# Attention's end and the first branch stage: weights split sooner, loads and splits in program order

## The chip, the core and the metric

The kernel runs on one core of a Trainium2 chip. The metric is the device time of one execution in microseconds (us). The engines named below are TensorE (PE; PEld is its weight load), VectorE (DVE), ScalarE (ACT), GpSimd (POOL), and SyncE (SP), whose queue issues nearly all DMA transfers here. An engine works through its instructions strictly in the order in which they stand in its queue: if one waits, all behind it wait.

## The reference

One layer of a hybrid block over 2048 tokens of width 1024, batch 1, with 256 context tokens, all in float32. Cut to what matters here:

```python
attn_x = merge_heads(attend_blocked(q_x, k_all, v_all))            # 8 heads of 64, 2304 keys
gm_x = gmlp_spatial(gelu(u_x), gelu(vg_x), gm_norm_g, gm_ws, gm_bs)
y = sigmoid(ga_x) * (attn_x @ w_br_attn) + sigmoid(gb_x) * (gm_x @ w_br_gm)   # 512 -> 1024
x = x + g1 * (y @ w_out)                                           # 1024 -> 1024
h2 = modulate(x, norm2_g, sh2, sc2)
x = x + g2 * square(relu(h2 @ w_ff1)) @ w_ff2                      # 1024 -> 4096 -> 1024
```

The softmax of `attend` is divided by its sums late: the kernel stores unscaled attention outputs, the sums, and their reciprocals, and scales when the branch stage reads them.

## The kernel before

**Precision.** A float32 operand is split into a high part (a cast on ACT) and a remainder (a subtraction, here on DVE): `split`, lines 146 and 150. A product is three matmuls, `mm3`, lines 178 (high x high), 179 (high x remainder) and 180 (remainder x high). So the second operand of line 180 needs the remainder of the weight, line 178 only its cast.

**Stages.** Projection, attention, the branch stage with the output product (`merge`), then two feed-forward halves. Tokens come in four blocks of 512.

*Attention* is 16 units (a block and a pair of heads), each of 18 key blocks in three groups of six (`gi` 0 to 2). In a group TensorE does the scores (L1689), ACT the exponentials (L1699), and one group later TensorE the products with the values (L1709) while DVE or POOL add up the exponentials (L1729, L1732; for the last unit all on DVE, its final pair L1718). In the last unit there is no next unit to prepare, and in that time the raw branch weights of m=0 and m=1 (`br_raw`) are loaded and split (`br_weights`): these two sets are `self.ready`.

*The branch stage* of block b runs over m = 0 to 7, the eight 128-wide slices of y. For m, TensorE multiplies the gMLP branch ("g") and the attention branch ("a") by their weights, 12 matmuls each. DVE multiplies each by its gate (L985), adds them (L988), and ACT and DVE split the sum into `y`. Ahead of that, `fetch` loads and splits the weights of two slices later and loads their gates (`gate_in`, L950: `gt<-ta_d`, `gt<-tb_d`). Block 0's stage carries three more things: `load_w_out` loads the eight slices of the output weights (`ws`, L875, 512 KB each) and splits them into `wo`; `last.sums` forms the softmax sums of the last attention unit at m=2; and `last.inverse` turns them into reciprocals through DRAM at m=4 (load L1769, DVE L1770, store L1771).

*The output product* then goes over the four 128-token tiles of the block, two halves of 512 columns each, k = 0 to 7 over the slices of y and `wo`. The first tile runs k = 0 to 6 of both halves first and k = 7 last, so that the last slice may come late. DVE multiplies by g1 (L1032) and adds x (L1033, loaded by L1012), SP stores the result (L1035). Meanwhile the next block's inputs are fetched and split (`br_inputs`, L884, L888, L896).

**Buffers.** At the end of attention the pools `base` and `mid` are closed and `out` and `branch` are opened in the same memory; a tile of a new pool waits for the last user of the bytes below it. `branch` holds 6 gate tiles (`gt`), 14 branch-weight tiles (`bw`; a set is 2 raw and 4 split tiles) and 2 raw output-weight tiles (`ws`). With two `ws` tiles, load k waits until slice k-2 is split. PSUM has 8 banks.

**What sets the order.** A planner puts each engine's instructions in an order of its own, by costs that it assumes, and wait instructions follow from the data. `order`, called at the end of the build, adds edges that hold ranges of the program to program order on their engine:

```python
held = idx in pinned or (idx in fixed and i.engine in engines)      # engines: PE, DVE
held = held or (idx in steady and i.engine != self.nc.sync.engine)  # all but SP
held = held or (idx in loads and i.engine == self.nc.sync.engine)   # SP
```

Attention is in `fixed` (PE and DVE in order, ACT and SP free). `steady` begins at the output product of block 0. Block 0's branch stage is in neither `steady` nor `loads`, so there every queue follows the planner. `loads` holds the second feed-forward product only.

Of the kernel before, what the change touches and what calls it, by code (L numbers as in the profile page):

```python
# [10 lines left out]
F32R = mybir.dt.float32r  # L11
# [7 lines left out]
P = 128  # L19
D = 1024  # L20
KC = D // P
SEQ = 2048
CTX = 256
NH = 8
# [5 lines left out]
TB = 512  # L30
NB = SEQ // TB
TT = TB // P
# [36 lines left out]
class Kern:  # L69
# [748 lines left out]
    def attend(self, units, late):  # L818
        begin = self.here()
        pend, self.ready = [], []  # L820
        for i, u in enumerate(units):
            at = lambda n: units[n] if 0 <= n < len(units) else None
            nxt, far, old, older = at(i + 1), at(i + 2), at(i - 1), at(i - 2)
            for gi, g in enumerate(range(0, NKT, GROUP)):
                group = range(g, g + GROUP)
                step = nxt if gi < 2 else far
                if not nxt and gi == 0:
                    raws = [self.br_raw(m, self.t2) for m in range(2)]
                for j in group:
                    u.scores(j)  # L830
                    if step:
                        step.maxima(1)
                    if gi == 0 and j == 2 and far:
                        far.load()
                if gi == 2 and nxt:
                    nxt.low_queries()
                if gi == 2 and i in FIRST_INPUTS:
                    next(late, None)
                for f in pend:
                    f()  # L840
                if gi == 1 and far:
                    far.queries()
                if gi == 0 and far:
                    far.cast()
                if gi == 2 and old:
                    old.sums()
                if gi == 0:
                    if older:
                        older.inverse()
                    if far:  # L850
                        far.remainder()
                if gi == 1:
                    if nxt:
                        nxt.reference()
                    if old:
                        old.join()
                if gi == 2 and i in FIRST_INPUTS:
                    next(late, None)
                if not nxt and gi:
                    self.ready.append(self.br_weights(raws.pop(0), self.t2))  # L860
                pend = [lambda u=u, j=j: u.values(j) for j in group]
            pend.append(u.leave)
        for f in pend:
            f()
        units[-2].inverse()
        self.fixed.append(range(begin, self.here()))

    def load_w_out(self):
        nc = self.nc
        self.wo = []  # L870
        self.g1b = self.sb("g1", [D])
        nc.sync.dma_start(self.g1b, self.g1_d.partition_broadcast(P)[:, 0, :])
        for k in range(KC):
            st = self.sb("ws", [D])
            nc.sync.dma_start(st, self.I["w_out"][0, k * P : (k + 1) * P, :])  # L875
            h, l = self.sb("wo", [D], F32R), self.sb("wo", [D], F32R)
            self.split(st, h, l, lo_eng="dve")
            self.wo.append((h, l))
            yield

    def br_fetch(self, b, nm, k):
# [72 lines left out]
    def merge(self, first, start, last):  # L954
        nc = self.nc
# [8 lines left out]
        w_out = self.load_w_out()  # L964

        def fetch():
            s = next(it, None)
            if s is not None:
                q.append((self.br_weights(self.br_raw(s[1])), self.gate_in(*s)))

        inp = first
        for ws in self.ready:
            q.append((ws, self.gate_in(*next(it))))
        for b in range(NB):
            y = []
            for m in range(KC):
                fetch()
                ws, gt = q.pop(0)
                for nm in ("g", "a"):
                    ps = self.bank([TB])  # L980
                    wh, wl = ws[nm]
                    for k in range(4):
                        h, l = inp[nm][k]
                        self.mm3(ps, wh[:, k, :], wl[:, k, :], h, l, k == 0, k == 3)
                    nc.vector.scalar_tensor_tensor(  # L985
                        out=gt[nm], in0=gt[nm], scalar=1.0, in1=ps, op0=ALU.add, op1=ALU.mult
                    )
                nc.vector.tensor_tensor(out=gt["a"], in0=gt["a"], in1=gt["g"], op=ALU.add)  # L988
                yh, yl = self.sb("y", [TB], F32R), self.sb("y", [TB], F32R)
                self.split(gt["a"], yh, yl, lo_eng="dve")  # L990
                y.append((yh, yl))
                if b == 0:
                    next(w_out, None)
                    if m == 2:
                        last.sums(self.sb("raw", [TB]))
                    if m == 4:
                        last.inverse()
            inp = {}
            if b == 0:
                begin = self.here()  # L1000
            if b + 1 < NB:
                side = self.br_inputs(b + 1, inp)
            else:
# [5 lines left out]
            for tt in range(TT):  # L1009
                tok = slice(tt * P, (tt + 1) * P)  # L1010
                xt = self.sb("xt", [D])
                nc.sync.dma_start(xt, self.x_block(b)[tok, :])  # L1012
                banks = [self.bank([512]) for _ in range(2)]

                def outer(n, ks):
# [569 lines left out]
class Unit:  # L1585
# [161 lines left out]
    def sums(self, row=None):  # L1747
# [10 lines left out]
        for h in range(2):  # L1758
            n = 2 * self.p + h
            nc.scalar.dma_start(k.sm_d[self.b][n : n + 1], row[h * HD : h * HD + 1])  # L1760

    def inverse(self):
        if self.p + 1 < NH // 2:
            return
        k, nc = self.k, self.nc
        n = NH * TT
        r = (k.sb("raw", [TB]) if self.last else k.t1([P]))[:n, :P]
        pack = lambda d: d.rearrange("h (t c) -> (h t) c", c=P)
        nc.sync.dma_start(r, pack(k.sm_d[self.b]))  # L1769
        nc.vector.reciprocal(r, r)  # L1770
        nc.sync.dma_start(pack(k.rs_d[self.b]), r)  # L1771


@with_exitstack
# [42 lines left out]
```

## Time and profile before

| | |
|---|---|
| median of 3 runs | 3013.18 us (3012.45 to 3016.2) |
| the profiled execution | 3012.34 us; span from first to last instruction 3010.6 us, granted clock 0.999 |
| TensorE busy | 2971.5 us, 99% of the span |
| DVE, ACT, POOL busy | 2024.5 us (67%), 1353.1 us (45%), 564.9 us (19%) |
| attention's last values product | ends near 1395.5 us |
| block 0's branch stage | 1395.5 us to about 1445 us |
| its output product | to about 1489 us |

How to read it: times in the profile are us from the span's start unless marked ns. A row of the timeline has start, length, engine, line, operation, output tile <- input tiles, shapes and count; the bracket at its end is how long the engine stood idle before it and what released it. "SPq" and "ACTq" are the DMA-issuing queues of SP and ACT. In a row of windows each engine's busy time is followed by its number of instructions; then come the granted TensorE clock (1.00 is full), the busy share of the DMA engines, and GB/s. A row of waits has the waiting engine and line, what it waited for, us in total, how often, and the longest. TensorE's matmuls overlap: a row's length is longer than the step from one to the next.

### The profile page before, as it was taken

The page shows a single profiled execution, that of the slowest core. Times are in us where ns is not written, and L with a number is a line of the kernel's source. Part 1 is how long each engine was busy: PE and PEld are TensorE (multiplying, and loading weights), DVE is VectorE, ACT ScalarE, POOL GpSimd, SP SyncE. Part 2 cuts the span into 40 slices and gives each one's busy share as a digit, 9 for nine tenths or more (in the row PEclk, how much of TensorE's full clock was granted, in tenths as well). Part 3 has the DMA queues.
Part 4 walks back from the last instruction along what each step waited for, and adds up shares of the span by engine and source line. Part 5 has one row for each costly group of instructions (what it writes and reads, how often), then busy time and mean ns, then how long its engine had stood idle before and what let it go on. Part 6 is the DMA issues. An engine that isn't in the chain of part 4 may idle for free.

```text
span 3010.6 us, 39824 instructions
## 1 busy us (share of the span) xinstructions
PE 2971.5 (99%) x14973; PEld 2300.4 (76%) x14973; DVE 2024.5 (67%) x2989; ACT 1353.1 (45%) x2041; POOL 564.9 (19%) x420
## 2 busy tenths in 40 slices
PE   7999999999999999999999999999999999999999
PEld 5888888887655656556888878887788888888887
DVE  5848566585777788886655688776755766654455
ACT  4444435342655555554322355443543344444442
POOL 0000000000888899980000000000000000000000
PEclk9999999999999999999999999999999999999999
DMA  7474646643100000003755549888766544446665
GB/s 239 124 219 118 225 137 198 180 138 98 36 15 12 15 19 22 29 26 131 234 174 179 173 151 328 310 305 312 243 203 226 183 154 154 154 148 219 209 218 195
DMA packets 329123, 485.53 MB, mean 161 GB/s; under 512 B 28825, under 2 KB 161217, under 8 KB 328930
## 3 DMA queue, kind: packets, MB, share of 16 engines
q1 hardware_dynamic: 325090, 478.40, 48.1%
q10 hardware_dynamic: 3840, 4.59, 0.4%
q8 instruction: 117, 1.92, 0.3%
q14 instruction: 76, 0.62, 0.1%
HBM read 348.56 MB, written 134.35 MB: 160 GB/s over the span
## 4 chain that ended last, share of the span: by engine, by line
PE 95%; DVE 2%; DMA 2%; ACT 1%; issue 1%; SPq 0%; DVEq 0%; ACTq 0%
PE b L1287 13%; PE b L1288 13%; PE b L1286 13%; PE b L178 11%; PE b L180 11%; PE b L179 11%; PE b L1689 9%; PE b L1709 8%; PE b L1645 2%; PE b L184 2%; DMA w<-in_w_mod 1%; PE b L1751 0%; PE b L288 0%; DMA f<-x_d 0%; DVE ts L1656 0%
## 5 line engine op out<-in xcount | busy, mean ns | idle before, releaser
L1392 DVE TENSOR_TENSOR f<-f,f 128x1024 fp32r<-128x1024 f32 x224 | 264.5, 1221 | 252.7 <-ACT f L1391 252.4
L1656 DVE TENSOR_REDUCE ts<-b 128x1 f32<-128x512 f32 x512 | 311.6, 682 | 105.6 <-PE b L1645 105.5
L1287 PE MATMUL b<-f,f 128*128 128x512 f32 x896 | 350.6, 391 | 5.5 <-DVE f L1392 5.3
L1391 ACT CAST f<-f 128x1024 fp32r<-128x1024 f32 x224 | 224.8, 1052 | 287.3 <-PE b L1287 274.8
L1286 PE MATMUL b<-f,f 128*128 128x512 f32 x896 | 350.2, 391 | 1.3 <-ACT f L1391 1.3
L1288 PE MATMUL b<-f,f 128*128 128x512 f32 x896 | 349.4, 390 | 0.0
L1689 PE MATMUL b<-t,t 64*128 64x512 f32 x2304 | 330.7, 400 | 0.0
L1689 PEld LDWEIGHTS b<-t,t 64*128 64x128 f32 x2304 | 226.1, 184 | 69.2 <-issue 26.1
L1732 POOL TENSOR_TENSOR ac<-ac,p 128x512 f32<-128x512 f32 x204 | 269.0, 1353 | 43.4 <-ACT p L1699 43.4
L1732 POOL TENSOR_TENSOR ac<-ac,t 128x512 f32<-128x512 f32 x146 | 233.2, 1627 | 0.0
L1699 ACT ACTIVATE p<-b 128x512 f32<-128x512 f32 x384 | 206.8, 599 | 48.2 <-PE b L1689 41.4
L1287 PE MATMUL b<-hl,f 128*128 128x512 f32 x576 | 224.4, 390 | 1.8 <-DVE hl L1049 1.8
L1288 PE MATMUL b<-hl,f 128*128 128x512 f32 x576 | 224.1, 389 | 0.0
L1286 PE MATMUL b<-hl,f 128*128 128x512 f32 x576 | 224.1, 389 | 0.0
L150 DVE TENSOR_TENSOR w<-w,w 128x1024 fp32r<-128x1024 f32 x120 | 146.7, 1223 | 113.5 <-ACT w L146 85.7
L178 PE MATMUL b<-t,w 128*128 128x512 f32 x512 | 203.2, 397 | 0.4 <-DVE ts L1651 0.3
L1287 PEld LDWEIGHTS b<-f,f 128*128 128x128 f32 x896 | 168.5, 188 | 44.1 <-DVE f L1392 9.5
L180 PE MATMUL b<-t,w 128*128 128x512 f32 x512 | 199.7, 390 | 0.0
L179 PE MATMUL b<-t,w 128*128 128x512 f32 x512 | 199.5, 390 | 0.0
L1286 PEld LDWEIGHTS b<-f,f 128*128 128x128 f32 x896 | 168.6, 188 | 37.3 <-ACT f L1391 2.4
L1288 PEld LDWEIGHTS b<-f,f 128*128 128x128 f32 x896 | 168.6, 188 | 34.7
L146 ACT CAST w<-w 128x1024 fp32r<-128x1024 f32 x120 | 125.9, 1049 | 146.5 <-DMA w<-in_w_in 116.8
(234 smaller groups left out, 6013.3 us busy)
## 6 DMA issues: line engine op xcount, KB each, us to landing
w<-in_w_in SPq DMA_DIRECT2D x120, 512.0 KB
ao_d<-f SPq DMA_DIRECT2D x224, 256.0 KB
f<-ao_d SPq DMA_DIRECT2D x112, 512.0 KB
f<-w2o_d SPq DMA_DIRECT2D x112, 512.0 KB
f<-in_w_ff SPq DMA_DIRECT2D x48, 1024.0 KB
w2o_d<-f SPq DMA_DIRECT2D x112, 256.0 KB
md<-in_w_mod SPq DMA_DIRECT2D x32, 512.0 KB
f<-x_d SPq DMA_DIRECT2D x64, 256.0 KB
```

The source lines that it names most:

```text
L178: mm(ps, sh, mh, start=start, stop=False, skip_group_check=skip)
L179: mm(ps, sh, ml, start=False, stop=False, skip_group_check=skip)
L180: mm(ps, sl, mh, start=False, stop=stop, skip_group_check=skip)
L1286: mm(ps, wh, hh, start=start and k == 0, stop=False, skip_group_check=True)
L1287: mm(ps, wh, hl, start=False, stop=False, skip_group_check=True)
L1288: mm(ps, wl, hh, start=False, stop=k == len(w) - 1, skip_group_check=True)
L1391: nc.scalar.copy(h, f32(l))
L1392: nc.vector.tensor_tensor(out=l, in0=f32(l), in1=f32(h), op=ALU.subtract)
L1656: nc.vector.tensor_reduce(out=self.mx[:, t, h, c : c + 1], in_=ps[h], axis=AX.X, op=ALU.max)
L1689: self.nc.tensor.matmul(ps[h], keys[h], q[rows[h]], start=n == 0, stop=n == len(steps) - 1, skip_group_check=True,)
L1709: nc.tensor.matmul(self.o[h * HD : (h + 1) * HD, :], k.V[c][:, i, self.kv * HD : (self.kv + 1) * HD], pt[h], start=j == 0, stop=j == NKT - 1,)
L1732: nc.gpsimd.tensor_tensor(out=self.acc[e][:, h], in0=old[:, h], in1=pt[h], op=ALU.add)
```

## The change

Four edits that belong together:

- In the last attention unit the two early branch-weight sets are split after groups 0 and 1, not 1 and 2.
- `load_w_out` issues the load of slice k and then the split of slice k-1, instead of load and split of the same slice; it is stepped twice at m=2 and m=3 (once at every other m), so its last split comes at m=6.
- The reciprocals are formed in two parts: `inverse_in` (the load) at m=4 and `inverse_out` (reciprocal and store) at m=6. The other blocks' reciprocals do both at once as before.
- `begin` moves ahead of block 0's branch stage. So `steady` now holds PE, ACT, DVE and POOL in program order there, and `loads` holds SP in program order from the first gate loads to the end of the stage. The x loads of block 0's output product are pinned, each behind the SP instruction ahead of it in the program.

```diff
--- before.py
+++ after.py
@@ -856,7 +856,7 @@
                         old.join()
                 if gi == 2 and i in FIRST_INPUTS:
                     next(late, None)
-                if not nxt and gi:
+                if not nxt and gi < 2:
                     self.ready.append(self.br_weights(raws.pop(0), self.t2))
                 pend = [lambda u=u, j=j: u.values(j) for j in group]
             pend.append(u.leave)
@@ -870,12 +870,15 @@
         self.wo = []
         self.g1b = self.sb("g1", [D])
         nc.sync.dma_start(self.g1b, self.g1_d.partition_broadcast(P)[:, 0, :])
-        for k in range(KC):
-            st = self.sb("ws", [D])
-            nc.sync.dma_start(st, self.I["w_out"][0, k * P : (k + 1) * P, :])
-            h, l = self.sb("wo", [D], F32R), self.sb("wo", [D], F32R)
-            self.split(st, h, l, lo_eng="dve")
-            self.wo.append((h, l))
+        st = []
+        for k in range(KC + 1):
+            if k < KC:
+                st.append(self.sb("ws", [D]))
+                nc.sync.dma_start(st[k], self.I["w_out"][0, k * P : (k + 1) * P, :])
+            if k:
+                h, l = self.sb("wo", [D], F32R), self.sb("wo", [D], F32R)
+                self.split(st[k - 1], h, l, lo_eng="dve")
+                self.wo.append((h, l))
             yield
 
     def br_fetch(self, b, nm, k):
@@ -969,6 +972,7 @@
                 q.append((self.br_weights(self.br_raw(s[1])), self.gate_in(*s)))
 
         inp = first
+        begin = self.here()
         for ws in self.ready:
             q.append((ws, self.gate_in(*next(it))))
         for b in range(NB):
@@ -990,14 +994,17 @@
                 self.split(gt["a"], yh, yl, lo_eng="dve")
                 y.append((yh, yl))
                 if b == 0:
-                    next(w_out, None)
+                    for _ in range(2 if m in (2, 3) else 1):
+                        next(w_out, None)
                     if m == 2:
                         last.sums(self.sb("raw", [TB]))
                     if m == 4:
-                        last.inverse()
+                        last.inverse_in()
+                    if m == 6:
+                        last.inverse_out()
             inp = {}
             if b == 0:
-                begin = self.here()
+                self.loads.append(range(begin, self.here()))
             if b + 1 < NB:
                 side = self.br_inputs(b + 1, inp)
             else:
@@ -1010,6 +1017,8 @@
                 tok = slice(tt * P, (tt + 1) * P)
                 xt = self.sb("xt", [D])
                 nc.sync.dma_start(xt, self.x_block(b)[tok, :])
+                if b == 0:
+                    self.pins.append((self.here() - 1,))
                 banks = [self.bank([512]) for _ in range(2)]
 
                 def outer(n, ks):
@@ -1759,16 +1768,22 @@
             n = 2 * self.p + h
             nc.scalar.dma_start(k.sm_d[self.b][n : n + 1], row[h * HD : h * HD + 1])
 
+    def inverse_in(self):
+        k = self.k
+        self.sm = (k.sb("raw", [TB]) if self.last else k.t1([P]))[: NH * TT, :P]
+        self.nc.sync.dma_start(self.sm, self.packed(k.sm_d))
+
+    def inverse_out(self):
+        self.nc.vector.reciprocal(self.sm, self.sm)
+        self.nc.sync.dma_start(self.packed(self.k.rs_d), self.sm)
+
+    def packed(self, d):
+        return d[self.b].rearrange("h (t c) -> (h t) c", c=P)
+
     def inverse(self):
-        if self.p + 1 < NH // 2:
-            return
-        k, nc = self.k, self.nc
-        n = NH * TT
-        r = (k.sb("raw", [TB]) if self.last else k.t1([P]))[:n, :P]
-        pack = lambda d: d.rearrange("h (t c) -> (h t) c", c=P)
-        nc.sync.dma_start(r, pack(k.sm_d[self.b]))
-        nc.vector.reciprocal(r, r)
-        nc.sync.dma_start(pack(k.rs_d[self.b]), r)
+        if self.p + 1 == NH // 2:
+            self.inverse_in()
+            self.inverse_out()
 
 
 @with_exitstack
```

## The prediction

> **What bounds the kernel now.** I read the page's busy shares first, then the windows around the change, then each engine's timeline there, then the waits of the DMA-issuing queue SP.
>
> ```profile
> PE 2971.5 (99%) x14973; PEld 2300.4 (76%) x14973; DVE 2024.5 (67%) x2989; ACT 1353.1 (45%) x2041; POOL 564.9 (19%) x420
> ...
> core 0: us, PE busy (x) PEld busy (x) DVE busy (x) ACT busy (x) POOL busy (x), PEclk, DMA share, GB/s
> 1395.00:1480.00 85.00, 81.73 (x353) 64.44 (x350) 57.84 (x82) 28.39 (x43) 0.00 (x0) 1.00 0.76 254
> ...
> 1395.47 0.50 PE L178 MATMUL b<-in,t 128*128 128x512 f32 x1
> ...
> 1407.97 0.50 PE L178 MATMUL b<-in,bw 128*128 128x512 f32 x1 [1.08 <-ACT bw L146]
> ...
> 1410.08 0.51 PE L180 MATMUL b<-in,bw 128*128 128x512 f32 x1 [1.36 <-DVE bw L150]
> ...
> 1433.24 0.50 PE L178 MATMUL b<-in,bw 128*128 128x512 f32 x1 [0.31 <-ACT bw L146]
> ...
> 1434.60 0.50 PE L180 MATMUL b<-in,bw 128*128 128x512 f32 x1 [0.35 <-DVE bw L150]
> ...
> 1439.84 0.50 PE L178 MATMUL b<-in,bw 128*128 128x512 f32 x1 [0.17 <-ACT bw L146]
> ```
>
> TensorE is busy 99% of the span; only its idle time can be won. Block 0's branch stage runs from 1395.47 us; in its window TensorE has 85 - 81.73 = 3.27 us of idle, which is the sum of the five bracketed gaps: 1.08 and 1.36 before the third branch weight (m=2), and 0.31, 0.35 and 0.17 before m=6 and m=7. So 3.27 us, 0.11%, is all the change can win here. POOL is not busy in the stage and no edit issues on it.
>
> ```profile
> SPq L950 <- DVE ac L1729: 78.2, 1, 78.2
> SPq L875 <- DVE wo L150: 6.9, 4, 2.3
> ...
> 1399.32 0.34 SPq L950 DMA_DIRECT2D gt<-ta_d  x1
> ...
> 1401.61 0.51 SPq L934 DMA_DIRECT2D bw<-in_w_br_gm  x1
> ...
> 1390.94 0.62 ACT L146 CAST t<-t 128x512 fp32r<-128x512 f32 x1
> ...
> 1407.31 1.14 ACT L146 CAST bw<-bw 128x512 fp32r<-128x512 f32 x2 [2.34 <-DMA bw<-in_w_br_gm]
> ...
> 1391.60 1.40 DVE L150 TENSOR_TENSOR t<-t,t 128x512 fp32r<-128x512 f32 x2 [12.58 <-ACT t L146]
> ...
> 1397.94 1.23 DVE L1729 TENSOR_TENSOR ac<-ac,t 128x1024 f32<-128x1024 f32 x1
> ```
>
> SP stands idle until its first gate load at 1399.32, released by attention's last sums on DVE (L1729, ends 1399.17). Those were late because DVE waited 12.58 us, in order, for the cast of the second early branch weight (ACT, 1390.94). The third weight, issued at 1401.61, is cast at 1407.31, 0.4 us after TensorE wanted it. From then on SP waits for output-weight splits (L875 behind `wo`).
>
> **The change, part by part.**
>
> *Branch weights a group sooner.* Four casts and four remainders move, nothing is added: 4 x 0.62 us on ACT, 4 x 0.69 us on DVE, now after the first and second groups of the last unit.
>
> ```profile
> 1367.57 0.59 ACT L1739 COPY t<-b 128x512 f32<-128x512 f32 x1 [3.71 <-PE b L1709]
> ...
> 1383.54 2.15 ACT L1699 ACTIVATE t<-b 128x512 f32<-128x512 f32 x4
> ...
> 1359.97 1.23 DVE L1729 TENSOR_TENSOR ac<-p,p 128x1024 f32<-128x1024 f32 x1 [2.78 <-ACT p L1699]
> ...
> 1393.65 1.89 PE L1709 MATMUL b<-t,t 128*64 128x512 f32 x8
> ```
>
> They cost nothing: ACT is idle 3.71 us before 1367.57 and DVE 2.78 us before 1359.97; without that cover TensorE could lose at most the casts' 2.5 us. The last group's exponentials end at 1385.7, so its six sums (1.25 us each) and the final pair end near 1388.5 instead of 1400.5. What holds the gate tile next is TensorE reading the same exponentials: the row at 1393.65 covers the last two key blocks, the first of them done near 1394.7. I take SP's first load there, 4.6 us sooner (at the earliest 1390.5, when the last group's first products are done; at the latest 1395.6). The third weight then lands near 1402.7, before TensorE wants it at 1406.9: the gaps of 1.08 and 1.36 go, a gain of 2.44 us.
>
> *Block 0's stage in order.* Now ACT, DVE and SP keep program order in it. Per m: SP loads the raw weights of m+2, then their gates, then `w_out`; DVE does both remainders of m+2, then m's two gate products, their sum, y's remainder, then the output-weight remainders. What is late next is whatever stands behind the slowest of these. Block 1, already in order on ACT and DVE, gives the chain's length:
>
> ```profile
> 1492.88 1.13 ACT L146 CAST bw<-bw 128x512 fp32r<-128x512 f32 x2
> ...
> 1493.51 1.29 DVE L150 TENSOR_TENSOR bw<-bw,bw 128x512 fp32r<-128x512 f32 x2 [0.87 <-ACT bw L146]
> 1494.72 1.28 DVE L985 SCALAR_TENSOR_TENSOR gt<-gt,b 128x512 f32<-128x512 f32 x2
> 1496.04 0.69 DVE L988 TENSOR_TENSOR gt<-gt,gt 128x512 f32<-128x512 f32 x1
> ...
> 1497.47 0.69 DVE L150 TENSOR_TENSOR y<-gt,y 128x512 fp32r<-128x512 f32 x1 [0.74 <-ACT y L146]
> ...
> 1425.41 1.22 DVE L150 TENSOR_TENSOR wo<-ws,wo 128x1024 fp32r<-128x1024 f32 x1
> ...
> 1419.67 0.33 SPq L875 DMA_DIRECT2D ws<-in_w_out  x1
> ...
> 1420.53 0.50 SPq L934 DMA_DIRECT2D bw<-in_w_br_gm  x1
> ...
> 1425.26 1.15 ACT L146 CAST bw<-bw 128x512 fp32r<-128x512 f32 x2
> ...
> 1427.56 0.46 SPq L934 DMA_DIRECT2D bw<-in_w_br_gm  x1
> ...
> 1432.57 1.14 ACT L146 CAST bw<-bw 128x512 fp32r<-128x512 f32 x2 [0.51 <-DMA bw<-in_w_br_gm]
> ```
>
> From the first cast (1492.88) to y's remainder (ends 1498.16) it takes 5.3 us; an output-weight remainder behind it adds 1.3 us. A branch weight takes 4.7 us from the issue of its second half to its cast (1420.53 to 1425.26), or 5.0 (1427.56 to 1432.57).
>
> *Output weights behind.* `next(w_out)` is called twice at m=2 and m=3, and each split now stands one call behind its load. There are two `ws` buffers, so load k waits for split k-2. Loads 3 and 5, the second of their pair, therefore wait for splits 1 and 3, which are the first output splits of the same m, at the end of that m's chain. Behind them in SP's order stand the raw weights of the next m. I follow it:
>
> An m is 24 matmuls, 5.7 us on TensorE: two of them run from 1395.47 to 1406.89. The sums at m=2 take 1 us more.
>
> - m=0, 1: weight 2 lands at 1402.7, y0 is done 5.3 us later at 1408.0 and frees the tile for gate load 3. Behind that go output load 1 and weight 4 (issued 1409.0 and 1409.4, landing 1414.1).
> - m=2: 1414.1 + 5.3 + 1.3 = 1420.7 for split 1, then load 3, weight 5 (1421.2 and 1421.6; before: 1420.53 for the second), landing 1426.3. TensorE, 2.44 us sooner than before, wants it at 1406.9 + 3 x 5.7 + 1 = 1425.0 and gets its cast 0.6 us after the landing: 1.9 us lost.
> - m=3: DVE stands behind weight 5 although the products of m=3 are long done. 1426.3 + 5.3 + 1.3 = 1432.9 for split 3, then load 5, weight 6 (second half 1433.8), landing 1438.5. Before, split 3 ran at 1425.41 without waiting for weight 5, and weight 6 was out at 1427.56. TensorE ends m=5 at 1432.6 and starts m=6 at 1439.1: 6.5 us lost.
> - m=4, 5: weight 7 stands behind no late split; DVE paces. 1438.5 + 6.6 = 1445.1 (split 5, which frees load 7 and behind it weight 8: second half 1446.0, landing 1450.7).
> - m=6: 1450.7 + 6.6 = 1457.3 (split 7).
>
> *The reciprocal in two parts.* The sums' load moves to SP at m=4, where its 16 KB cost one issue slot and the source was stored long before. The reciprocal and the store come at m=6, behind split 7 on DVE:
>
> ```profile
> 1431.87 0.93 DVE L1770 RECIPROCAL raw<-raw 32x128 f32<-32x128 f32 x1
> ...
> 1432.84 0.32 SPq L1771 DMA_DIRECT2D rs_d<-raw  x1
> ...
> 1455.87 0.69 DVE L1032 TENSOR_TENSOR jk<-b,g 128x512 f32<-128x512 f32 x1 [1.08 <-PE b L180]
> ```
>
> 1457.3 + 0.9 = 1458.2, then the store, then weight 9 (for block 1, m=1; second half 1459.1), landing at 1463.8. DVE's order puts its remainders ahead of m=7's products, so y7 is ready at 1463.8 + 5.3 = 1469.1. Overlap can only shorten this: DVE's operations follow each other at 0.60 us where I count 0.69, and weight 9 finds an empty queue. I take 2 us off for it: 1467. TensorE needs y7 for the last k of the first output tile. Before, it ran that step about 0.7 us ahead of the row at 1455.87, from 1455.2. So TensorE is 11.8 us late there; earlier losses lie inside this one.
>
> *The x loads of block 0* are pinned behind their predecessors on SP. Tile tt's load then follows the store of tt-1; VectorE's residual waits perhaps 1 us, four pairs of banks cover that, cost 0; uncovered, 1 us a tile, 3 us.
>
> *The clock.*
>
> ```profile
> 2180.00:2184.00 4.00, 2.17 (x8) 1.26 (x7) 3.75 (x6) 4.00 (x6) 0.00 (x0) 0.95 0.41 157
> 2184.00:2187.00 3.00, 3.00 (x8) 2.32 (x8) 3.00 (x6) 1.89 (x4) 0.00 (x0) 0.50 0.89 272
> 2187.00:2190.00 3.00, 3.00 (x14) 2.44 (x14) 2.91 (x4) 0.17 (x1) 0.00 (x0) 1.00 0.73 252
> ```
>
> After 1.83 us of idle within 4 us, TensorE ran at half clock: 8 matmuls in 3 us where the next 3 us have 14, so 6 x 0.23 = 1.4 us lost. Gaps of 2.44 us at 1407 cost none of it. After a wait of over 6 us I count one drop, at y7; that of m=6 disappears in the wait behind it. The Trainium skill, "TensorE: Matmul & The Clock Gate", Part 1, says that one idle window of about 3.4 us halves the clock; by that rule both long waits cool it and the sum keeps its 1.4 us, while by the gaps at 1407 alone it would be 11.8 us.
>
> **Sum.** +11.8 + 1.4 = 13.2 us, against the profiled execution's 3012.34 us: 3025.5 us. The median of the runs stands 0.84 us above it, less than the spread of those three runs (3.75 us). I forecast 3025.5 us, +0.44%. For this kernel 0.2%, 6.0 us, is about what a measurement can tell.
>
> Bounds of the forecast: SP's start at 1390.5 takes up to 4.2 us off, at 1395.6 it adds 0.9; a landing 0.7 us quicker or slower in each of the four transfers in the chain (weights 5, 6, 8, 9) is 2.8 us either way; the clock 1.4 us either way. Together about +6 to +18, 3018.3 to 3030.3 us.
>
> **Rivals.**
>
> - *The queue hardly stands still, and only the gain is left* (the other side). The place is SP's wait before output load 5. Before, four such waits of L875 took 6.9 us together and at most 2.3. If they stay that short, weight 6 goes out by 1426, TensorE meets it ready at 1431, and the win of 2.44 to 3.27 us remains: 3009.1 to 3009.9. For it: DVE was busy only 57.84 of the stage's 85 us, and the DMA engines 0.76. Against it: the chain hangs on waits, not on load. It decides from a wait of about 3 us; each further one is lost on TensorE. Split 1 hardly moves, though:
>
> ```profile
> 1418.41 1.23 DVE L150 TENSOR_TENSOR wo<-ws,wo 128x1024 fp32r<-128x1024 f32 x1 [1.38 <-ACT wo L146]
> ```
>
>   with DVE free to choose its order it ran then, so load 3 cannot come much sooner. Chance 0.13.
> - *The reciprocal's loop hides.* If split 7 is done some 10 us sooner than I have it, y7 is ready in time, and the loss is that of m=5 and m=6 with one clock drop less the win of before: 1.9 + 6.5 + 1.4 - 3.3 = 6.5 us, or 5.1 without the drop: 3017.4 to 3018.8. For it: the store is one of the smallest transfers. Against it: weight 9 stands behind it whatever its size. Chance 0.10.
> - *Nothing moves*: the queues' old order equals the new one. The order of SP before (load 3 ahead of weight 5, load 5 ahead of weight 6) speaks for it; ACT's and DVE's speak against it. 3012.3, chance 0.03.
> - *Transfers land sooner.* If each of the four weights in the chain lands 1.5 us sooner than the rows have it, because its queue is emptier than in the trace, y7 gains 6 us and the sum is +7: 3019.5, inside the forecast; 0.06 of its chance. The Trainium skill speaks for this one: "DMA: Bandwidth & Descriptors", Anatomy of one DMA, fits a transfer (on the GpSimd path, not SP's) as 2.0 us plus bytes at 436 GB/s, an estimate of 3.2 us for a weight's 512 KB. The rows at 1420.53 and 1427.56 disagree with 4.7 and 5.0 us, and they decide.
>
> **How the numbers follow.** Forecast 0.74 with the fourth rival in it; it and the upper end of the second rival are slower by over 0.2%: 0.75. Faster by over 0.2% would take 6 us where 3.27 are idle: 0.02. Within: 0.23. The range leaves out the gains (0.13) and some 0.05 at the top: 3011 to 3031 us.
>
> **What would show it.** Right: SP's first gate load near 1394.7 and no wait before weight 2; on SP a long wait of L875 behind `wo` twice, near 1420 and 1432 (some 5 us or more each); TensorE waiting some 6 us for `bw` at m=6, and some 6 us for `y` before the first output tile's last k; weight 9 issued right behind the store of the reciprocals. Wrong: DVE products of m=3 ahead of weight 5's remainders, or weight 6 issued before 1429. The forecast falls if SP does not stand still behind output loads 3 and 5.

## The result and the profile after

The changed kernel takes 3030.25 us (median of 4 runs, 3029.21 to 3031.66) against 3012.89 us (4 runs, 3012.45 to 3016.2) for the kernel before: ratio 1.0057, 95% interval 1.0044 to 1.0069. It is slower by 17.4 us, where 13.2 were forecast (3025.5 us, range 3011 to 3031). The profiled execution took 3029.21 us, 16.9 above that of before; its span is 3027.4 us, 16.8 longer. Lines have moved: the load of `ws` is now L877, the branch weights L937, the gates L953, the gate operations L989 and L992, the reciprocals L1774, L1777 and L1778.

First the page's busy row:

```profile
PE 2975.6 (98%) x14973; PEld 2304.2 (76%) x14973; DVE 2025.3 (67%) x2989; ACT 1352.4 (45%) x2041; POOL 564.5 (19%) x420
```

Then the row of the window 1395 to 1500 us, its columns as before:

```profile
1395.00:1500.00 105.00, 89.21 (x368) 70.76 (x365) 54.51 (x77) 29.23 (x46) 0.00 (x0) 0.93 0.64 205
```

And what TensorE waited for between 1380 and 1500 us (us in total, times, longest):

```profile
PE b L178 <- ACT bw L146: 10.0, 2, 5.4
PE b L178 <- ACT y L146: 5.8, 1, 5.8
```

TensorE's work is the same; what is new is 15.8 us of waiting in block 0's branch stage and output product, where 3.27 us stood before. That is 12.5 us more; to this comes what is lost to the clock, whose mean in this window is 0.93 instead of 1.00 (the windows at half clock stand in the last section). The waiting falls in three pieces, in the timeline of TensorE:

```profile
1429.08 0.80 PE L178 MATMUL b<-in,bw 128*128 128x512 f32 x1 [4.64 <-ACT bw L146]
...
1441.60 0.80 PE L178 MATMUL b<-in,bw 128*128 128x512 f32 x1 [5.38 <-ACT bw L146]
...
1470.13 0.80 PE L178 MATMUL b<-wo,y 128*128 128x512 f32 x1 [5.77 <-ACT y L146]
```

The first matmul of m=5, that of m=6 and the last k of the first output tile start late. At m=2 there is no bracket any more, so the 2.44 us of before are gone. SP's timeline shows what stood in front of the weights (L937; the second half of a set is `in_w_br_gm`); a row "x2" with a long duration is two loads, the second of which waited:

```profile
1401.34 0.34 SPq L953 DMA_DIRECT2D gt<-tb_d  x1
...
1416.92 6.32 SPq L877 DMA_DIRECT2D ws<-in_w_out  x2
...
1423.81 0.46 SPq L937 DMA_DIRECT2D bw<-in_w_br_gm  x1
...
1425.39 10.11 SPq L877 DMA_DIRECT2D ws<-in_w_out  x2
...
1461.37 0.32 SPq L1778 DMA_DIRECT2D rs_d<-raw  x1
...
1462.25 0.46 SPq L937 DMA_DIRECT2D bw<-in_w_br_gm  x1
```

SP's waits between 1380 and 1500 us:

```profile
SPq L877 <- DVE wo L150: 16.2, 4, 8.5
...
SPq L1778 <- DVE raw L1777: 8.8, 1, 8.8
...
SPq L953 <- DMA at_d<-t: 2.9, 1, 2.9
SPq L953 <- PE b L1718: 2.0, 1, 2.0
```

The two loads of `ws` behind m=2 end at 1423.2, those behind m=3 at 1435.5, and weights 5 and 6 go out right after them; the store of the reciprocals (1461.37) has waited 8.8 us and weight 9 goes out right behind it. The other half of the loop is on DVE, in its timeline:

```profile
1421.66 2.36 DVE L150 TENSOR_TENSOR wo<-ws,wo 128x1024 fp32r<-128x1024 f32 x2 [0.25 <-ACT wo L146]
1429.06 1.29 DVE L150 TENSOR_TENSOR bw<-bw,bw 128x512 fp32r<-128x512 f32 x2 [5.05 <-ACT bw L146]
...
1433.92 2.36 DVE L150 TENSOR_TENSOR wo<-ws,wo 128x1024 fp32r<-128x1024 f32 x2 [0.26 <-ACT wo L146]
...
1466.21 1.29 DVE L150 TENSOR_TENSOR bw<-bw,bw 128x512 fp32r<-128x512 f32 x2 [4.87 <-ACT bw L146]
...
1470.12 0.69 DVE L150 TENSOR_TENSOR y<-gt,y 128x512 fp32r<-128x512 f32 x1 [0.68 <-ACT y L146]
```

DVE stands 5.05 us for weight 5, with everything of m=3 behind it, and only then reaches splits 3 and 4 (1433.92), the first of which frees the buffer that SP waits for in front of weight 6. So SP stands for DVE and DVE for SP's load. A turn takes 4.6 us for the load (1423.81 to the cast at 1428.41) and 7 from the cast until SP goes on (1435.5); TensorE does an m in 5.7.

At the end of attention, DVE's timeline (the sums, L1729 before, are L1738 now) shows that its long wait for a cast has moved and not gone:

```profile
1368.74 1.29 DVE L150 TENSOR_TENSOR t<-t,t 128x512 fp32r<-128x512 f32 x2 [11.54 <-ACT t L146]
...
1391.48 1.23 DVE L1738 TENSOR_TENSOR ac<-ac,t 128x1024 f32<-128x1024 f32 x1
```

It is 11.54 us now, ahead of the sums of the last unit's first group, where it was 12.58 us ahead of the last group's. The sum that SP waits for ends at 1392.7 instead of 1399.17. Then SP waits 2.0 us more, for TensorE (L1718, the products with the values), and the first gate load goes out at 1394.79.

### The profile page after: what moved, and what is told of

Read it like the earlier page. It is cut to its first block, busy times and chain, and to the rows that moved or that the text cites. A ratio compares the mean times of both kernels' runs of the same rounds, so it can differ in the third digit from the quotient of the medians.

```text
span 3027.4 us, 39823 instructions
## 1 busy us (share of the span) xinstructions
PE 2975.6 (98%) x14973; PEld 2304.2 (76%) x14973; DVE 2025.3 (67%) x2989; ACT 1352.4 (45%) x2041; POOL 564.5 (19%) x420
## 4 chain that ended last, share of the span: by engine, by line
PE 94%; DMA 2%; DVE 2%; ACT 1%; issue 1%; SPq 0%; DVEq 0%; ACTq 0%
PE b L1296 13%; PE b L1295 13%; PE b L1297 13%; PE b L178 11%; PE b L180 11%; PE b L179 11%; PE b L1698 9%; PE b L1718 8%; PE b L1654 2%; PE b L184 2%; DMA bw<-in_w_br_gm 1%; DMA w<-in_w_mod 1%; PE b L1760 0%; PE b L288 0%; DMA f<-x_d 0%
## 5 line engine op out<-in xcount | busy, mean ns | idle before, releaser
L178 PE MATMUL b<-w,t 128*128 128x512 f32 (+1 forms) x528 | 191.5, 363 | 0.2 <-DVE t L148 0.2
```

What stands on the lines that cost most here:

```text
L178: mm(ps, sh, mh, start=start, stop=False, skip_group_check=skip)
```

## The experiments

Three theories were set against each other. A: SP in program order stands with the branch weights behind it, twice for a staging buffer and once for the reciprocals. B: it is the order of the compute engines, DVE's above all, that makes the splits late. C: the pinned x loads. The runs of before beside the experiments have medians of 3013.83 (the first four), 3013.55 (the next four), 3013.16 and 3013.55 us.

**Four staging buffers.** `"ws": 2` becomes `"ws": 4`; all else as changed.

> The changed kernel with four raw output-weight tiles instead of two, so that output load k waits for split k-4 and loads 3 and 5 find free tiles; every order is kept. Theory A (SP stands still behind output loads 3 and 5, and later behind the reciprocals' store): the two waits of TensorE for branch weights at m=5 and m=6 (4.6 and 5.4 us) go, the wait for the last slice of y (5.8 us) stays, the last slice comes some 10 to 12 us sooner; 3017 to 3020 us. Theory B (the program order on DVE and ACT costs the time, SP's waits only follow from it): DVE keeps its order, so under 3 us of change, 3027 to 3030 us. Theory C (the pinned x loads or something behind the stage): no change, 3030 us.

3019.59 us, ratio 1.0021 (1.0011 to 1.0030). SP's timeline, then TensorE's:

```profile
1421.70 1.43 SPq L877 DMA_DIRECT2D ws<-in_w_out  x2
...
1459.54 0.80 PE L178 MATMUL b<-wo,y 128*128 128x512 f32 x1 [5.62 <-ACT y L146]
```

The pair of loads that took 10.11 us on SP takes 1.43, no wait for `bw` above 0.8 us is left, and the wait for y before the last k stays at 5.62. So the two long waits of L877 cost 10.7 us of the 17.

**The reciprocals last.**

```diff
-                    if m == 6:
-                        last.inverse_out()
             if b == 0:
+                last.inverse_out()
```

> The changed kernel with the reciprocal and its store behind m=7 instead of m=6, so that branch weight 9 no longer stands behind the store on SP. Theory A: the wait for the last slice of y (5.8 us) goes with its clock drop (1.4 us), the waits at m=5 and m=6 stay; 3022 to 3024 us. Theory B: weight 9 was late because DVE was, so under 2 us of change, 3028 to 3030 us. Theory C: 3030 us.

3024.99 us, 1.0041 (1.0026 to 1.0056). TensorE's timeline:

```profile
1458.75 0.50 PE L178 MATMUL b<-wo,y 128*128 128x512 f32 x1 [0.40 <-ACT y L146]
...
1506.16 0.80 PE L178 MATMUL b<-in,bw 128*128 128x512 f32 x1 [2.08 <-ACT in L146]
```

The wait before the last k shrinks from 5.77 to 0.40 us; those for `bw` stay (3.56 and 4.36 us). But block 1's first input is late now, 2.08 us, as the later store lets one expect: of what is won at one place a part is lost at the next. The gain is 5.3 us, and the time lies 1 us above the 3022 to 3024 us of theory A; the runs of the two kernels do not overlap (3024.49 to 3027.48 us against 3029.21 to 3031.66).

**SP free, compute engines in order.** The line `self.loads.append(range(begin, self.here()))` is left out.

> The changed kernel without holding SP to program order in block 0's branch stage; DVE, ACT and TensorE stay in program order. Theory A: the planner puts weights 5, 6 and 9 ahead of output loads or the store, as it did before for some; most of the loss goes, 3010 to 3018 us. Theory B: the compute queues' order is the cause, so most of the loss stays, 3023 to 3030 us. Theory C: 3030 us.

3014.36 us, 1.0004 (0.9994 to 1.0013). SP's timeline:

```profile
1417.76 0.43 SPq L937 DMA_DIRECT2D bw<-in_w_br_attn  x1
```

And TensorE's waits from 1380 to 1500 us:

```profile
PE b L178 <- ACT bw L146: 3.9, 3, 2.1
```

The planner puts weight 5 between loads 2 and 3, 5.5 us before the changed kernel issues it, and 3.9 us of waits are left. The x loads keep their pins here, so C has nothing to explain.

**Compute engines free, SP in order.** `begin = self.here()` stands once more behind `loads.append`, so `steady` begins after the stage.

> The changed kernel without holding DVE, ACT and TensorE to program order in block 0's branch stage; SP stays in program order. Theory A: SP still stands behind output loads 3 and 5, but splits 1 and 3 can run before the branch weights' remainders, so the waits shrink without going: 3013 to 3022 us. Theory B: the whole loss goes, 3010 to 3012 us. Theory C: 3030 us.

3014.45 us, 1.0003 (0.9993 to 1.0012). The timelines of SP, TensorE and DVE:

```profile
1415.40 7.66 SPq L877 DMA_DIRECT2D ws<-in_w_out  x2
...
1425.66 3.50 SPq L877 DMA_DIRECT2D ws<-in_w_out  x2
...
1409.96 0.50 PE L180 MATMUL b<-in,bw 128*128 128x512 f32 x1 [2.73 <-DVE bw L150]
...
1427.57 1.23 DVE L150 TENSOR_TENSOR wo<-ws,wo 128x1024 fp32r<-128x1024 f32 x1 [0.57 <-ACT wo L146]
...
1429.32 0.68 DVE L150 TENSOR_TENSOR bw<-bw,bw 128x512 fp32r<-128x512 f32 x1
```

SP still stands 7.66 us at loads 2 and 3, but DVE now does split 3 at 1427.57, ahead of weight 5's remainders (1429.32) and not behind them: SP's two loads there take 3.50 us instead of 10.11, and the loop ends there. This time and the one before it lie in theory A's ranges and in neither of B's. Yet A as worded is too narrow as well: SP in order costs almost nothing once DVE may run split 3 first. The loss needs both orders; freeing either one opens the loop. And DVE, free, takes the first products before the third weight's remainders, which brings a wait of 2.73 us back at m=2.

**Four buffers and the reciprocals last.** Both edits together.

> The changed kernel with four buffers for the output weights' staging and with the reciprocal and its store behind the last unit instead of behind m = 6, so both edits tried singly before are together. Theory 'two ordered queues' (the two waits of SyncE for a staging buffer and its wait for the reciprocal each hold the weight loads behind them, and nothing else is lost): the waits for bw go as with four buffers alone (0.25 to 0.80 us each were left), the wait before the last k goes as with the reciprocal last alone (0.40 us left), and block 1's first input may be waited for by about 2 us, as there. 3030 - 10.7 - 5.3 = 3014 us, 3012 to 3016. Rival 'the two losses overlap' (a single late queue is counted twice): one of the two waits comes back in another place and the time stays over 3017 us.

3015.53 us, 1.0006 (0.9997 to 1.0014), so the two gains add up, 16 us expected and 14.7 found; the longest wait of TensorE between 1380 and 1520 us is 0.93 us, for block 1's first input.

**The early weights alone.** The kernel before with `gi < 2` for `gi`, nothing else. (The sets meant are those of m=0 and m=1, split in the last unit.)

> The kernel before with one part of the change alone: the branch weights of the third and fourth unit are split one third of a unit sooner (the condition with gi < 2); the order of block 0's branch stage stays the planner's. Theory 'the earlier start is a gain of its own': the 2.44 us of gaps at m = 2 are gone and the time is 3010.5 to 3012 us. Rival 'the gaps come back': with the planner's order VectorE takes the first products before the weights' low parts, as where the compute engines were free of the order (2.73 us at m = 2 there), and the time is 3013 to 3014.5 us, no different from before.

3013.50 us, 1.0001 (0.9992 to 1.0010): the rival holds. DVE's timeline (L985 is the gate product, as before), then TensorE's:

```profile
1407.16 1.28 DVE L985 SCALAR_TENSOR_TENSOR gt<-gt,b 128x512 f32<-128x512 f32 x2 [3.56 <-PE b L180]
...
1409.57 1.29 DVE L150 TENSOR_TENSOR bw<-bw,bw 128x512 fp32r<-128x512 f32 x2
...
1410.31 0.50 PE L180 MATMUL b<-in,bw 128*128 128x512 f32 x1 [2.73 <-DVE bw L150]
```

The cast of the weight now is there in time, but DVE does the gate products (L985) and two more operations first, and line 180 waits 2.73 us for the remainder, where the two gaps of before had 2.44. Without an order for DVE the earlier weight is worth nothing.

**The old loader in the new order.** Load k and split k in the same step again, one step for each m; buffers, orders and reciprocals as changed.

```diff
-        for k in range(KC + 1):
-            if k < KC:
-                st.append(...)          # load k
-            if k:
-                ...                     # split k - 1
+        for k in range(KC):
+            ...                         # load k, then split k
...
-                    for _ in range(2 if m in (2, 3) else 1):
-                        next(w_out, None)
+                    next(w_out, None)
```

> The changed kernel with the old loader of the output weights: load k and split k stand in the same step and one step follows each m, instead of load k one step ahead of split k-1 with two steps behind m = 2 and m = 3. Everything else of the change is kept, two staging buffers and both orders included. Theory 'two ordered queues': a load no longer stands in SyncE's queue ahead of the split that frees its buffer by more than a step, so the waits for bw at m = 5 and m = 6 vanish (under 1.5 us together), and the wait of about 5.5 to 7 us before the last k, which hangs on the reciprocal's store, stays: 3018 to 3021 us. Rival 'the ordered stage itself is slow' (any order written out for SyncE with two buffers loses as much): 3026 to 3031 us.

3019.65 us, 1.0021 (1.0012 to 1.0030). TensorE's timeline:

```profile
1460.07 0.80 PE L178 MATMUL b<-wo,y 128*128 128x512 f32 x1 [3.29 <-ACT wo L146]
```

And of SP's waits that for the reciprocals (L1774 is the store in this kernel):

```profile
SPq L1774 <- DVE raw L1773: 8.1, 1, 8.1
```

With two buffers and both orders kept, the waits for `bw` are gone. So it is the loader, load k ahead of split k-1 and two steps behind m=2 and m=3, that closes the loop, not the order as such. The wait that the store causes stays, but before the last k TensorE now waits for `wo`, whose last load stands behind the store as weight 9 does; 3.29 us, or 4.8 with a wait of 1.49 us for `wo` ahead of it, where 5.5 to 7 were expected.

**The old loader and the reciprocals last.** Both edits.

> As the kernel with the old loader, and the reciprocal with its store behind the last unit as well. Theory 'two ordered queues': all four waits are gone but for some 1 to 3 us, plus a wait of about 2 us for block 1's first input as with the reciprocal last before: 3011.5 to 3015 us, so with both orders kept and two staging buffers the loss is nearly all gone. Rival 'the ordered stage itself is slow': over 3020 us.

3013.70 us, 0.9999 (0.9990 to 1.0008): inside what the two ordered queues give, with a wait of 1.5 us for block 1's input.

**The store on another queue.** In the next two kernels block 0's store of the reciprocals is issued by ACT and the reciprocal keeps its place behind m=6, first with the old loader, then in the changed kernel.

```diff
-        self.nc.sync.dma_start(self.packed(self.k.rs_d), self.sm)
+        eng = self.nc.scalar if self.last else self.nc.sync
+        eng.dma_start(self.packed(self.k.rs_d), self.sm)
```

> As the kernel with the old loader of the output weights, and block 0's store of the reciprocals is issued from ScalarE's queue instead of SyncE's; the reciprocal stays behind m = 6. If it is SyncE standing in front of the weight loads that costs the time (two ordered queues), the wait of 4.8 us at the end of block 0's stage goes although the reciprocal itself is as late as before: 3012 to 3015 us, and without the wait for block 1's first input (1.5 us with the reciprocal last). Rival 'the reciprocal's place on VectorE is the cost': the wait stays and the time is 3018 to 3021 us. Rival 'ScalarE stands instead': ScalarE waits for VectorE with the casts behind it, a wait for bw or wo of 2 to 5 us comes up and the time is 3015 to 3018 us.

3013.58 us, 1.0004 (0.9995 to 1.0013). The timelines of TensorE and ACT:

```profile
1447.98 0.50 PE L178 MATMUL b<-wo,y 128*128 128x512 f32 x1 [0.76 <-ACT wo L146]
...
1449.24 0.50 PE L179 MATMUL b<-wo,y 128*128 128x512 f32 x1 [0.76 <-DVE wo L150]
...
1450.48 1.14 ACT L146 CAST bw<-bw 128x512 fp32r<-128x512 f32 x2 [2.55 <-DVE raw L1773]
```

ACT does stand for DVE, 2.55 us before the casts at 1450.48, but nothing needs those at once. The wait of 3.29 us before the last k is gone though the reciprocal is as late in DVE's order as before: what cost time was SP standing in front of loads.

> The changed kernel with only the queue of block 0's store of the reciprocals changed, from SyncE's to ScalarE's. Two ordered queues: the waits of 4.6 and 5.4 us for bw at m = 5 and m = 6 stay, since the loads that stand for a staging buffer are untouched; the wait of 5.8 us for y before the last k shrinks to under 1.5 us: 3023 to 3026 us. Rival 'the reciprocal's place on VectorE': nothing changes, 3029 to 3031 us.

3025.53 us, 1.0039 (1.0026 to 1.0051). TensorE's timeline:

```profile
1467.18 0.50 PE L178 MATMUL b<-wo,y 128*128 128x512 f32 x1 [2.03 <-ACT y L146]
```

The waits for `bw` stay (4.5 and 4.4 us); the last wait is 2.03 us (1.5 was expected at most) instead of 5.77.

**The store of attention's values on another queue.** SP's row at 1401.34 has a wait that the prediction did not have: 2.9 us for ACT's store of `at_d`, with which the gate load shares no data. In the trace's instruction records both transfers count on the same DMA semaphore (number 101), and the gate load waits for it. Here that one store is issued by GpSimd.

```diff
-        self.nc.scalar.dma_start(k.at_d[...], oc)
+        (self.nc.gpsimd if self.last else self.nc.scalar).dma_start(k.at_d[...], oc)
```

> The changed kernel with the last attention unit's store of its values (at_d, issued by ScalarE at 1396.23 us, landed at 1401.33) on GpSimd's queue instead of ScalarE's; all else and all orders stay. In the changed kernel SyncE stood 2.9 us for that store, in front of a gate load, the first output-weight load and the branch weight of m = 3. If this wait is a semaphore that the two queues' transfers share and it made the stage later than forecast (output split 1 at 1422.9 instead of 1420.7), then the wait is gone, the weight of m = 3 is issued near 1400.3 instead of 1403.2, the remainders of weight 4 no longer stand behind split 0, and from the wait at m = 5 (2.5 to 3.5 us instead of 4.64) on everything is 1 to 2.2 us sooner: 3028 to 3029 us. Rival 'the queue of DMA is busy then': the gate load lands as late whatever queue the store has, the wait turns up on the next load, and the time stays 3030 to 3031 us.

3029.63 us, 1.0051 (1.0039 to 1.0064), above the 3028 to 3029 us expected; the difference to the changed kernel, 0.6 us, is not resolved. The stage is clear in the timelines of SP and TensorE:

```profile
1398.15 0.53 SPq L953 DMA_DIRECT2D gt<-tb_d  x1
...
1401.67 0.38 SPq L937 DMA_DIRECT2D bw<-in_w_br_gm  x1
...
1427.15 0.50 PE L178 MATMUL b<-in,bw 128*128 128x512 f32 x1 [2.73 <-ACT bw L146]
...
1468.44 0.79 PE L178 MATMUL b<-wo,y 128*128 128x512 f32 x1 [5.84 <-ACT y L146]
```

The wait is gone: the gate load goes out at 1398.15 instead of 1401.34. GpSimd issued the store at 1396.47 and it landed 5.0 us later, so the load did not need the store to be done, for its data or for the memory under its tile. Weight 3 goes out at 1401.67 instead of 1403.16 (1400.3 was expected), and the last k starts 1.7 us sooner. The rival is out. A part went back to the clock, in the window in which it is at half after the last wait:

```profile
1466.40:1473.20 6.80, 4.75 (x11) 3.75 (x12) 5.00 (x9) 1.66 (x3) 0.00 (x0) 0.50 0.58 178
```

It ends 4.8 us after TensorE's start at 1468.44; in the changed kernel it was 2.9 us. The profiled execution, 3032.42 us, also loses time behind the stage: its granted clock is 0.97 from 2100 to 2150 us, where the changed kernel's is 1.00. So the gain is shown in the stage alone.

**All together.** The old loader, the store on ACT, four buffers and the `at_d` store on GpSimd.

> The best that the runs point to: the old loader of the output weights, the store of the reciprocals on ScalarE's queue, and besides four staging buffers and the last store of attention's values on GpSimd's queue. The waits for wo of 0.76, 0.76 and 0.67 us that were left with the first two edits go, and with them the drop of the clock that followed them: if the 2.44 us of the third branch weight are a gain of their own, 3010 to 3012 us, still inside what five rounds can tell from no change. Rival 'the gain comes back elsewhere' (block 1's inputs, or VectorE's products first): 3013 to 3015 us.

3014.78 us, 1.0003 (0.9994 to 1.0012): above the 3010 to 3012 us expected and within the rival's 3013 to 3015, though the waits are not where the rival put them. The waits for `wo` did not go:

```profile
1453.71 0.50 PE L178 MATMUL b<-wo,y 128*128 128x512 f32 x1 [1.21 <-ACT wo L146]
```

Load k and split k in one step put the last split close to its use, and four waits of TensorE, 3.2 us together, take the place of the 3.27 us of before. No version tried beats the kernel before by more than its measurement can tell.

## Why the prediction was right, and where it was off

The mechanism was the forecast one, but for the steps named below; its sum was 3.7 us short of the profiled execution. The steps, in us; the last column is the kernel with the `at_d` store on GpSimd's queue:

| step | forecast | changed | without the wait for `at_d` |
|---|---|---|---|
| SP's first gate load | 1394.7 | 1394.79 | 1394.76 |
| weight 4, second half issued | 1409.4 | 1410.39 | 1409.68 |
| weight 5, second half issued | 1421.6 | 1423.81 | 1422.08 |
| TensorE's wait at m=5 | 1.9 | 4.64 | 2.73 |
| weight 6, second half issued | 1433.8 | 1436.07 | 1434.13 |
| m=6 starts | 1439.1 | 1441.60 | 1439.37 |
| weight 8, second half issued | 1446.0 | 1448.59 | 1446.37 |
| weight 9, second half issued | 1459.1 | 1462.25 | 1460.50 |
| y7 done | 1469.1 by rows, 1467 taken | 1470.81 | 1469.11 |

- *Branch weights sooner.* Right in what it gives: SP starts when forecast, the gaps at m=2 are gone, and TensorE waits nowhere at the end of attention, so the moved operations cost nothing. Not right on the way there: the last sums and the final pair were to end near 1388.5, and the pair ended at 1394.1. DVE was still busy with the group before when the last exponentials were done, for it had stood 11.54 us for the casts of the first set, where the forecast counted on 2.78 us of idle time as cover. It did not matter, because SP waited for TensorE 2.0 us longer than for DVE; the agreement of SP's start is in part luck. And "the gaps of 1.08 and 1.36 go" holds only together with the order on DVE, as the kernel with the early weights alone shows.
- *Output weights behind.* Right in kind and place, and confirmed by itself: four buffers take out 10.7 us. The terms ran 2.2 to 3.2 us late from weight 5 on. The step that failed is m=0 and 1, which follows weights 2 and 4 and leaves out weight 3. SP stood for `at_d`, weight 3 went out at 1403.16 and was cast at 1410.10, m=1's chain came late on DVE, and split 0 (1415.67) stood in front of weight 4's remainders (1416.81). Without that wait, the issues agree with the forecast to 0.5 us down to weight 8, and the wait at m=5 to 0.8.
- *The reciprocal in two parts.* Right that weight 9 stands behind the store and y7 behind weight 9; moving only the store to another queue takes out 4.7 us. Wrong was "I take 2 us off": the undiscounted 1469.1 is what the stage gives without the wait for `at_d`. That it fits so well is luck, though: in that kernel weight 8 took 5.6 us from its issue to its cast and weight 9 took 3.4, where 4.7 were counted for each, and the two errors cancel. One reason given for the discount, that weight 9 lands sooner, came true; weight 8 took back what it gave.
- *The sum.* The last k starts at 1470.13. Before, its first matmul started at 1454.99 and not at the 1455.2 of the forecast, so it is 15.1 us late, where 11.8 were forecast: of the 3.3 between, 2.1 is the discount, 1.7 is y7 at 1470.81 instead of 1469.1, which goes with the wait for `at_d`, 0.2 is the start of before, and 0.7 goes off again, because line 178 needs only the cast of y7 and not the remainder. With the half clock behind it, from 1470.13 to 1473.03, half of 2.9 us, it is 16.6 of the 16.8 us by which the span grew.
- *The bounds.* The measured median, 3030.25 us, lies just under the upper bound of 3030.3. The terms named for the lower bound add up to 8.4 us below the sum, so it should have been +4.8 us and not +6.
- *The clock.* One drop at y7 was counted, at 1.4 us, and that is its size. There are two more, behind the waits at m=5 and m=6, and they are hidden in the waits that follow, as was said of that at m=6.
- *The x loads.* Cost 0, as forecast; with SP free and the pins kept, no loss is left to measure.
- *The rivals.* "The queue hardly stands still": the four waits of L877 are 16.2 us with a longest of 8.5, far above its 3 us. "The reciprocal's loop hides": y7 was not in time, TensorE waited 5.77 us for it. "Nothing moves": the time moved by 17.4 us. "Transfers land sooner": the weights in the chain took 4.6, 4.9, 5.2 and 3.3 us from the second half's issue to the cast. The last cast, on ACT in the changed kernel:

```profile
1465.56 1.14 ACT L146 CAST bw<-bw 128x512 fp32r<-128x512 f32 x2 [6.33 <-DMA bw<-in_w_br_gm]
```

Weight 9 came near the 3.2 us that the forecast estimated from the Trainium skill ("DMA: Bandwidth & Descriptors", Anatomy of one DMA); the three others did not, so the rows decide here. Weights 6 and 9 both went out after a long stand of SP (8.5 and 8.8 us), but 5, 6 and 8 each went out right behind a 512 KB output load, and 9 behind the 16 KB store. That this makes the difference was not tested by itself.

## What to carry to other kernels

When two engines are both held in program order, look for a loop: a transfer that waits for a buffer, the engine that frees it, and the transfer queued behind the first that this engine waits for; each turn costs a whole transfer and a whole chain of operations. In this case more buffers (four for two), a load issued in the step that uses it, or one queue left free each broke it, and a store that waits for a result was better on a queue with no loads behind it. An estimate made of rows should keep its rows' sum: a discount for what may overlap needs a row of its own.

## What the runs showed of the chip

**The clock drops on a grid.** The rows below are windows of the changed kernel in steps of 3.41 us, laid so that the changes of the granted clock fall on their bounds.

```profile
1425.25:1428.66 3.41, 0.00 (x0) 0.00 (x0) 0.00 (x0) 0.25 (x1) 0.00 (x0) 1.00 1.02 319
1428.66:1432.07 3.41, 2.99 (x7) 2.37 (x8) 2.97 (x5) 0.89 (x2) 0.00 (x0) 0.50 0.51 205
...
1435.49:1438.90 3.41, 0.73 (x4) 0.27 (x2) 0.79 (x1) 0.00 (x0) 0.00 (x0) 1.00 0.79 231
1438.90:1442.31 3.41, 0.71 (x2) 0.50 (x2) 0.73 (x2) 1.14 (x2) 0.00 (x0) 0.50 1.01 354
...
1462.80:1466.21 3.41, 1.56 (x7) 0.95 (x6) 0.00 (x0) 0.65 (x2) 0.00 (x0) 1.00 0.91 270
1466.21:1469.62 3.41, 0.00 (x0) 0.00 (x0) 3.18 (x5) 0.65 (x2) 0.00 (x0) 1.00 0.97 294
1469.62:1473.03 3.41, 2.90 (x7) 2.28 (x8) 1.87 (x3) 1.50 (x3) 0.00 (x0) 0.50 0.87 278
```

And two of the kernel with the old loader and the store on ACT:

```profile
1446.41:1449.82 3.41, 1.90 (x8) 1.03 (x7) 2.55 (x3) 1.52 (x2) 0.00 (x0) 1.00 0.68 201
1449.82:1453.23 3.41, 3.41 (x10) 2.63 (x9) 2.32 (x5) 1.14 (x2) 0.00 (x0) 0.50 0.99 357
```

The changes of the clock in this stage of the changed kernel lie whole multiples of 3.413 us apart (1428.66 to 1473.03 is 13 of them), and a drop lasts one step, or two where the window in between was mostly idle (0.71 us busy in 1438.90 to 1442.31). That fits the free-running window of 3413 ns of the Trainium skill, "TensorE: Matmul & The Clock Gate", Part 1. Its rule of one idle window, which the prediction weighed, covers the drops at 1428.66 and 1469.62, behind windows with nothing in them. It does not cover the others: with 0.73 us busy in 1435.49 to 1438.90 the clock fell, and with 1.90 us busy in 1446.41 to 1449.82, two waits of 0.76 us, it fell too. Yet 1.56 us busy in 1462.80 to 1466.21 did not bring it down. Where the limit lies stays open.

**A queue can stand for another queue's transfer.** SP waited 2.9 us for a store of ACT that has no data in common with its load; both count on one semaphore, and with the store still under way on another queue the load went out without it. Moving the store to GpSimd's queue removed the wait and 1.7 us of the stage's delay.
